# Second half of an output projection, begun beside the last attention head and in the scores' PSUM banks

## The chip, the core and the metric

One core of a Trainium2 chip runs the whole step as one program. The metric is the time of one execution on the device in microseconds (us), the median over runs. The engines of the core are PE (matrix products), DVE and ACT (elementwise work, both read PSUM), POOL and SP (here mostly starters of transfers). PE writes into PSUM, which has eight banks of 128 x 512 numbers in f32.

## The reference

One layer of a streaming encoder on 1024 new rows, 16 meta rows and a sample stream of 32 rows with 512 cached positions (T = 1072 columns in the kernel, the rows being held transposed). Cut to what matters:

```python
mixed = concat(heads_A, heads_B)          # 8 latent heads (MLA), 8 forgetting heads (FoX), 64 wide
x = x + mixed @ w_out                     # output projection, 1024 x 1024
h = rms_norm(x, norm_ffn)
x = x + (silu(h @ w_gate) * (h @ w_up)) @ w_down      # 1024 -> 2816 -> 1024
y = rms_norm(x, norm_final)
```

All products are in f32 quality: an operand is split into a high and a low part (`hi`, `lo`), and each product is three matmuls, hi*hi, hi*lo and lo*hi.

## The kernel before

The program goes through four stages: input projections; the eight forgetting heads (8 to 15 in the code); the eight latent heads (0 to 7); and the rest of the output projection with the feed-forward part. A scheduler of the framework sets the order of the instructions on each engine from the order of the code, from the dependences and from the buffers; it may move an instruction past others that it does not depend on. Each engine then executes its list strictly in that order, and waits on semaphores stand in the list.

**Heads.** `attention` (L725) runs the heads. For each head `scores` (L560) computes nine tiles of scores, L589, into a tile `psS` of two banks, takes the maximum on DVE (L592) and the exponential on ACT (L597). `values` (L619) transposes the probabilities on PE (L651 and L627, into `psT`), copies them on ACT (L67 in the helper `split`, L655), subtracts on DVE (L68, L656), and multiplies by the head's values (L667, L668, L665, L637) into `po`. ACT and DVE bring the sum to `raw` (L675, L678, L680). After each second head `finish_pair` (L684) multiplies by the reciprocal row sums (transposed by L706, product L712) and splits the result into `A_hi` and `A_lo` (L713, L715). The values of a head run behind its scores as a generator, `state["pend"]`, whose steps alternate with the scores of the next group. The values of the last head's second group have nothing behind them, and run out at the end of the stage.

**Filler.** PE would wait in these chains, so a generator of other work is advanced by `fill` (L728). For the latent heads it is `out_half` (L537): the first half of the output projection, over the four blocks `B` of `mixed`, in 48 steps of six matmuls (L551 to L553), added to the input on DVE (L556) and put to DRAM as `sX2`. The rate is 48 steps over 25 x (8 - 0.7) calls; what is left at the start of the last head is run at once (L742).

**Second half.** After the pools of the heads are closed, 24 units (8 blocks of outputs `m`, times the column chunks `FC` of 408, 408 and 256) multiply the blocks `A` of `mixed`, k = 0 to 3, by `w_out` (L845 to L847). Four units at a time do k = 0 to 2 and then k = 3; `A`'s block k = 3 belongs to the last two heads. Their accumulators come from `psG`, a pool of six single banks. DVE adds each to `x2` (L852), which SP loads from `sX2` (eight loads, L820), ACT squares it for the norm (L826, L829), and DVE and ACT make the feed-forward input in the buffers of `A` and `B` (L858, L859) and the factor `rb` (L110 to L116).

**Feed-forward part.** 22 blocks f of 128 hidden columns. For each of the three chunks `gate_up` (L865) makes the gate product and the up product, 24 matmuls each (L121 to L123 in `mm3`), in a bank each; DVE reads the gate bank (L877, times `rb`), ACT takes silu, DVE reads the up bank (L882), multiplies (L883) and splits (L68) into `ah`, `al`. Then `down` (L893) makes the eight down products of the block before, three matmuls each (L889 to L891), in a bank each, and DVE adds each to `x2` (L898). All draw from the six banks of `psG` in turn. DVE also splits the next block's weights (L68, `gl`, `dl`). The last block (f = 21) is laced with the final norm (`down_final`, L923).

```python
psG = C.enter_context(tc.tile_pool(name="psG", bufs=6, space=PSUM))
ps = psG.tile([128, 512], F32, tag="psG", name="psG")      # product(j) of gate_up, L870
```

Of the kernel before, what the change touches and what calls it, by code (L numbers as in the profile page):

```python
# [9 lines left out]
F32 = mybir.dt.float32  # L10
# [39 lines left out]
def trunk(ctx: ExitStack, tc: tile.TileContext, a):  # L50
# [53 lines left out]
    def rows4(t):  # L104
        return t.rearrange("p (k t) -> p k t", k=4)
# [330 lines left out]
    tp = B.enter_context(tc.tile_pool(name="tp", bufs=LAG + 1))  # L436
    st = B.enter_context(tc.tile_pool(name="st", bufs=2))

    psS = B.enter_context(tc.tile_pool(name="psS", bufs=2, space=PSUM))
    psT = B.enter_context(tc.tile_pool(name="psT", bufs=2, space=PSUM))  # L440
    psO = B.enter_context(tc.tile_pool(name="psO", bufs=1, space=PSUM))
    psF = B.enter_context(tc.tile_pool(name="psF", bufs=1, space=PSUM))
# [280 lines left out]
    state = {"pend": iter(()), "n": 0}  # L723

    def attention(hs, filler, steps, last):  # L725
        rate, owed = steps / (25.0 * (len(hs) - 0.7)), [0.0]

        def fill():  # L728
            if last and h == hs[0] and grps[0][0] == 5:
                return  # L730
            owed[0] += rate
            while owed[0] >= 1:
                next(filler, None)
                owed[0] -= 1

        rs = raw = None
        for h in hs:
            nxt = h + 1 if h + 1 < 16 else 0
            if not (last and h == hs[-1]):
                heads[nxt] = 0  # L740
            ops, v = heads.pop(h)
            if h == hs[-1]:  # L742
                for _ in filler:
                    pass
                if not last:
                    masks()
            nops = fetch(nxt) if nxt in heads else None
            if h % 2 == 0:
                rs = st.tile([128, 2, 9], F32, tag="rs", name="rs")
                pool.memset(rs, 1.0)  # L750
                raw = st.tile([128, T], F32, tag="raw", name="raw", bufs=1)
            for grps in (((5, 6, 7, 8),), ((1, 2, 3, 4), (0,))):
                todo = [i for g in grps for i in g]
                P, done = {}, 0
                for j, i in enumerate(todo):
                    P[i] = scores(h, ops, i, rs)
                    fill()
                    while done < (j + 1) * state["n"] // len(todo):
                        next(state["pend"], None)
                        fill()  # L760
                        done += 1
                for _ in state["pend"]:
                    pass
                if nops is not None and len(grps) == 1:
                    heads[nxt] = (nops, fetch_v(nxt))
                gens = [values(h, v, [(i, P[i]) for i in g], raw) for g in grps]
                state["n"] = sum(len(g) + g[0] if g != (0,) else 1 for g in grps)
                if h % 2 == 1 and len(grps) == 2:
                    gens.append(finish_pair(h // 2, rs, raw))
                    state["n"] += 3  # L770
                state["pend"] = chain(*gens)
        for _ in filler:
            pass
# [6 lines left out]
    def masks():  # L780
        B3 = rooms[-1][:106]
        for j, part in enumerate((0, 0, 1)):
            move(B3[32 * j:32 * j + 32], sKR[:, part])
        move(B3[96:106], sMK[0:10])
        mixed["B3"] = B3
# [2 lines left out]
    mixed["A"] = (slot("A_hi"), slot("A_lo"))  # L788

    attention(range(0, 8), out_half(), 48, True)  # L790
    for _ in state["pend"]:
        pass
    B.close()
    hpx.close()
# [2 lines left out]
    with ExitStack() as C:  # L797
# [1 line left out]
        sqp = C.enter_context(tc.tile_pool(name="sqpC", bufs=1, side="right"))  # L799
        ap_ = C.enter_context(tc.tile_pool(name="ap", bufs=2, side="right"))  # L800
        wf = C.enter_context(tc.tile_pool(name="wpf", bufs=2))
        psG = C.enter_context(tc.tile_pool(name="psG", bufs=6, space=PSUM))
        psN = C.enter_context(tc.tile_pool(name="psNF", bufs=2, space=PSUM))

        def ffn_weights(f):
            gh = wf.tile([128, 2, 8, 128], FR, tag="gh", name="gh")
# [23 lines left out]
                marks[1] = eng.tensor_tensor(out=acc[:, cs], in0=acc[:, cs], in1=sq[:, :n], op=ALU.add).ins  # L830

        big = [tuple(rows4(t) for t in mixed[g]) for g in ("A", "B")]
        m_hi, m_lo = big[0]
        W = None
        units = [(m, c) for m in range(8) for c in FC]
        for u0 in range(0, len(units), 4):
            part = []
            for m, (c0, n) in units[u0:u0 + 4]:
                out_weights(8 + m + 2)
                part.append((m, c0, n, psG.tile([128, 512], F32, tag="psG", name="psG"), w_ring[8 + m]))  # L840

            for ks in ((0, 1, 2), (3,)):
                for m, c0, n, ps, w in part:
                    for k in ks:
                        pe.matmul(ps[:, :n], w[0][:, k], m_hi[:, k, c0:c0 + n], start=(k == 0), stop=False)  # L845
                        pe.matmul(ps[:, :n], w[0][:, k], m_lo[:, k, c0:c0 + n], start=False, stop=False)
                        pe.matmul(ps[:, :n], w[1][:, k], m_hi[:, k, c0:c0 + n], start=False, stop=(k == 3))  # L847
            if u0 == 12:
                W = ffn_weights(0)
            for m, c0, n, ps, w in part:  # L850
                cs = slice(c0, c0 + n)
                dve.tensor_tensor(out=x2[:, m, cs], in0=ps[:, :n], in1=x2[:, m, cs], op=ALU.add)  # L852
                square(m, cs, n, dve)
                if m == 7:

                    for k in range(8):
                        hi, lo = (t[:, k % 4, cs] for t in big[k // 4])
                        act.activation(hi, x2[:, k, cs], AF.Copy, scale=g_ffn[:, k:k + 1])  # L858
                        dve.scalar_tensor_tensor(lo, x2[:, k, cs], g_ffn[:, k:k + 1], f32(hi), ALU.mult, ALU.subtract)  # L859
                    ps = psN.tile([128, 512], F32, tag="psn", name="psn")  # L860
                    pe.matmul(ps[:, :n], ones, acc[:, cs], start=True, stop=True)
                    rsqrt(rb[:, cs], ps, n, D, sqp)


        def gate_up(W, c0, n, ah, al, between=None):  # L865
# [1 line left out]
            cs = slice(c0, c0 + n)  # L867

            def product(j):
                ps = psG.tile([128, 512], F32, tag="psG", name="psG")  # L870
                marks[2] = mm3(ps[:, :n], lambda k: gh[:, j, k], lambda k: gl[:, j, k], lambda k: big[k // 4][0][:, k % 4, cs], lambda k: big[k // 4][1][:, k % 4, cs], 8)
                return ps

# [19 lines left out]
        def down(parts, c0, n, norm=False, then=None):  # L893
            cs = slice(c0, c0 + n)
            for m in range(8):
                ps = psG.tile([128, 512], F32, tag="psG", name="psD")
                down_mm(ps[:, :n], m, cs, parts, True, True)
                dve.tensor_tensor(out=x2[:, m, cs], in0=ps[:, :n], in1=x2[:, m, cs], op=ALU.add)  # L898
                if norm:
                    square(m, cs, n, pool if m < 6 else dve)  # L900
                if m == 3 and then is not None:
                    norm_table()
                    final(*then)
# [19 lines left out]
        def down_final(prev, cur, c0, n):  # L923

            cs = slice(c0, c0 + n)
            pairs = [psG.tile([128, 512], F32, tag="psG", name="psD").rearrange("p (a b) -> p a b", a=2) for _ in range(4)]
            for part in (prev, cur):

                with tc.issue_after(marks[2]):
# [159 lines left out]
```

## Time and profile before

| | |
|---|---|
| median of 3 runs | 1538.38 us (1536.78 to 1539.22) |
| the profiled execution | 1537.25 us, span of the trace 1535.5 us |
| PE busy | 1493.0 us (97%), 9317 matmuls |
| DVE busy | 971.5 us (63%) |
| ACT busy | 591.4 us (39%) |
| mean granted clock of PE | 0.993 |
| heads 0 to 7 | about 453 to 689 us |
| rest of the projection | 688.81 to 738.20 us |
| feed-forward part | from 738.20 us |

Times in the trace count from the start of the span. A row of the timeline has the start, the duration, the engine, the line, the operation with output and inputs, and in brackets the engine's idle time before it with what ended it. A matmul's row is longer than the distance to the next, since matmuls are pipelined. PEld is the load of a matmul's weights, which overlaps the matmul before it. The clock is the share of full speed that PE was granted.

### The profile page before, as it was taken

What the parts mean: (1) busy time and instruction counts of PE and PEld (TensorE: products, weight loads), DVE (VectorE), ACT (ScalarE), POOL (GpSimd) and SP (SyncE); (2) the same over time, 40 slices, a digit from 0 to 9 for tenths busy, and PEclk for the clock granted to TensorE, in tenths of its full rate; (3) what the DMA queues carried; (4) which work ended last, traced back from release to release, by engine and by line L of the source; (5) the groups of instructions that cost most, each with busy time, mean ns of one, the idle gap of its engine ahead of it and who ended that gap; (6) DMA issues with size and microseconds to landing.
All of it is one profiled execution on the core that took longest, in us unless ns stands there. A gap on an engine that the chain in (4) does not pass through costs nothing.

```text
span 1535.5 us, 24295 instructions
## 1 busy us (share of the span) xinstructions
PE 1493.0 (97%) x9317; PEld 1433.5 (93%) x9317; DVE 971.5 (63%) x1861; ACT 591.4 (39%) x1198; POOL 198.5 (13%) x331
## 2 busy tenths in 40 slices
PE   9999998999898999989999999999999999999996
PEld 8999997888787898979999999999999999999996
DVE  8874626787966776766855655555555555655547
ACT  7443436777655666654511111111111121111124
POOL 0343242422131211200000000000000000000001
PEclk9999999999999999999999999999999999999999
DMA  6689567778587686515111111111111111111003
GB/s 196 233 258 299 172 210 249 238 218 262 147 238 185 174 212 161 148 41 206 34 50 44 54 42 42 42 42 42 42 42 42 53 58 53 44 42 42 28 1 115
DMA packets 87636, 184.19 MB, mean 120 GB/s; under 512 B 9754, under 2 KB 52954, under 8 KB 87428
## 3 DMA queue, kind: packets, MB, share of 16 engines
q1 hardware_dynamic: 70592, 128.34, 28.8%
q0 software_dynamic: 16928, 54.29, 10.1%
q8 instruction: 74, 1.21, 0.3%
q14 instruction: 42, 0.34, 0.1%
HBM read 123.93 MB, written 58.67 MB: 119 GB/s over the span
## 4 chain that ended last, share of the span: by engine, by line
PE 88%; DVE 4%; ACT 3%; issue 2%; DMA 1%; POOL 1%; DVEq 0%; SPq 0%; POOLq 0%; ACTq 0%
PE psG L122 11%; PE psG L121 11%; PE psG L123 11%; PE psD L890 5%; PE psD L891 5%; PE psD L889 5%; PE psS L589 5%; PE psT L651 4%; PE psA L123 3%; PE psA L121 3%; PE psA L122 3%; PE po L667 2%; PE po L668 2%; PE psA L386 1%; PE psA L387 1%
## 5 line engine op out<-in xcount | busy, mean ns | idle before, releaser
L898 DVE TENSOR_TENSOR x<-psD,x 128x408 f32<-128x408 f32 (+1 forms) x496 | 236.2, 522 | 4.3 <-PE psD L891 4.3
L122 PE MATMUL psG<-B_lo,gh 128*128 128x408 f32 (+1 forms) x528 | 172.8, 327 | 0.0
L121 PE MATMUL psG<-B_hi,gh 128*128 128x408 f32 (+1 forms) x528 | 172.8, 327 | 0.0
L122 PE MATMUL psG<-A_lo,gh 128*128 128x408 f32 (+1 forms) x528 | 172.6, 327 | 0.0
L121 PE MATMUL psG<-A_hi,gh 128*128 128x408 f32 (+1 forms) x528 | 172.3, 326 | 0.0
L891 PE MATMUL psD<-ah,dl 128*128 128x408 f32 (+1 forms) x528 | 172.1, 326 | 0.0
L123 PE MATMUL psG<-B_hi,gl 128*128 128x408 f32 (+1 forms) x528 | 171.8, 325 | 0.0
L123 PE MATMUL psG<-A_hi,gl 128*128 128x408 f32 (+1 forms) x528 | 171.8, 325 | 0.0
L890 PE MATMUL psD<-al,dh 128*128 128x408 f32 (+1 forms) x528 | 171.7, 325 | 0.0
L889 PE MATMUL psD<-ah,dh 128*128 128x408 f32 (+1 forms) x528 | 170.9, 325 | 0.5 <-ACT ah L67 0.5
L878 ACT ACTIVATE sl<-sl 128x408 f32<-128x408 f32 (+1 forms) x66 | 33.1, 503 | 351.3 <-DVE sl L877 351.2
L882 DVE TENSOR_TENSOR sq<-psG,rb 128x408 f32<-128x408 f32 (+1 forms) x66 | 35.0, 530 | 156.5 <-PE psG L123 156.5
L68 DVE TENSOR_TENSOR ptl<-psT,pth 128x512 fp32r<-128x512 f32 x192 | 104.6, 552 | 28.7 <-ACT pth L67 26.6
L592 DVE TENSOR_REDUCE nm<-psS 128x1 f32<-128x656 f32 (+2 forms) x144 | 104.0, 724 | 27.2 <-PE psS L589 25.6
L67 ACT ACTIVATE pth<-psT 128x512 fp32r<-128x512 f32 (+4 forms) x208 | 99.2, 480 | 55.7 <-PE psT L651 46.5
L830 POOL TENSOR_TENSOR acc<-acc,sq 128x408 f32<-128x408 f32 x10 | 10.8, 1076 | 812.4 <-ACT sq L829 811.9
L877 DVE TENSOR_TENSOR sl<-psG,rb 128x408 f32<-128x408 f32 (+1 forms) x66 | 34.9, 530 | 123.0 <-PE psG L123 123.0
L67 ACT ACTIVATE ah<-sl 128x408 fp32r<-128x408 f32 (+1 forms) x66 | 33.2, 503 | 197.2 <-DVE sl L883 125.8
L589 PE MATMUL psS<-b,a 128*128 128x328 f32 (+4 forms) x360 | 99.9, 331 | 7.4 <-ACT pb L597 6.1
L889 PEld LDWEIGHTS psD<-ah,dh 128*128 128x128 f32 x528 | 99.2, 188 | 0.9 <-ACT ah L67 0.7
L122 PEld LDWEIGHTS psG<-B_lo,gh 128*128 128x128 f32 x528 | 99.2, 188 | 0.5 <-issue 0.3
L121 PEld LDWEIGHTS psG<-B_hi,gh 128*128 128x128 f32 x528 | 99.2, 188 | 0.5 <-issue 0.2
(274 smaller groups left out, 3803.5 us busy)
## 6 DMA issues: line engine op xcount, KB each, us to landing
sg<-w_gu SPq DMA_DIRECT2D x44, 512.0 KB
a<-sQ SPq DMA_DIRECT2D x56, 268.0 KB
b<-sK SPq DMA_DIRECT2D x32, 396.0 KB
sg<-w_down SPq DMA_DIRECT2D x22, 512.0 KB
v<-sV SPq DMA_DIRECT2D x16, 512.0 KB
wst<-w_in SPq DMA_DIRECT2D x13, 512.0 KB
sV<-vt POOLq DMA_DIRECT2D x24, 256.0 KB, 4.5
sK<-room POOLq DMA_DIRECT2D x14, 396.0 KB, 4.9
```

The source lines that it names most:

```text
L67: first = act.activation(hi, src, AF.Copy)
L68: return first.ins, eng.tensor_tensor(out=lo, in0=src, in1=f32(hi), op=ALU.subtract).ins
L121: pe.matmul(ps, whi(k), rhi(k), start=(k == 0), stop=False)
L122: pe.matmul(ps, whi(k), rlo(k), start=False, stop=False)
L123: last = pe.matmul(ps, wlo(k), rhi(k), start=False, stop=(k == K - 1))
L589: pe.matmul(out, qa[:K, t0:t0 + nq], kb[:K, k0 + c:k0 + c + w], start=(j == 0), stop=last)
L592: dve.tensor_reduce(out=nm[:nq, j:j + 1], in_=src, axis=AX.XY if len(src.shape) == 3 else AX.X, op=ALU.max, negate=True)
L651: pe.transpose(out=pt[:, 128 * g:128 * g + 128], in_=tiles[g][1][:, c:c + 128], identity=ident)
L889: pe.matmul(ps, dh[:, m], ah[:, cs], start=first and j == 0, stop=False)
L890: pe.matmul(ps, dh[:, m], al[:, cs], start=False, stop=False)
L891: pe.matmul(ps, dl[:, m], ah[:, cs], start=False, stop=last and j == len(parts) - 1)
L898: dve.tensor_tensor(out=x2[:, m, cs], in0=ps[:, :n], in1=x2[:, m, cs], op=ALU.add)
```

## The change

The pool `psS` of the scores, two tiles of two banks, now lives to the end of the program. A generator `begin` draws two of these tiles after the last head and runs k = 0 to 2 of the first four units into their four halves, one step after each step of the last head's values; the later loop does only k = 3 for them. For this the weight slices 8 and 9 of `w_out` are fetched there. `psG` shrinks to two banks, and a function `bank` deals out six banks in turn for everything that drew from `psG`: two halves of a `psS` tile, two halves of the other, two single banks. In `attention` the last range of heads no longer flushes the filler at its last head; its rate is 48 steps over 25 x (8 - 0.25) calls, and the rest runs after the loop.

```diff
-    psS = B.enter_context(tc.tile_pool(name="psS", bufs=2, space=PSUM))
+    psS = ctx.enter_context(tc.tile_pool(name="psS", bufs=2, space=PSUM))
...
-        rate, owed = steps / (25.0 * (len(hs) - 0.7)), [0.0]
+        rate, owed = steps / (25.0 * (len(hs) - (0.25 if last else 0.7))), [0.0]
...
-            if h == hs[-1]:
+            if h == hs[-1] and not last:
                 for _ in filler:
                     pass
-                if not last:
-                    masks()
+                masks()
...
+    def out_products(unit, ps, ks):
+        (m, (c0, n)), w = unit, w_ring[8 + unit[0]]
+        for k in ks:
+            for j, (wj, t) in enumerate(((0, 0), (0, 1), (1, 0))):
+                pe.matmul(ps[:, :n], w[wj][:, k], rows4(mixed["A"][t])[:, k, c0:c0 + n], start=(k == 0 and j == 0), stop=(k == 3 and j == 2))
+
+    early = []
+
+    def begin():
+        for u in (0, 2):
+            out_weights(10)
+            pair = psS.tile([128, 2, 512], F32, tag="psS", name="psS")
+            for j in range(2):
+                early.append(pair[:, j])
+                for k in range(3):
+                    out_products(units[u + j], pair[:, j], (k,))
+                    yield
+
+    begun = begin()
     for _ in state["pend"]:
+        next(begun, None)
+    for _ in begun:
         pass
...
-        psG = C.enter_context(tc.tile_pool(name="psG", bufs=6, space=PSUM))
+        psG = C.enter_context(tc.tile_pool(name="psG", bufs=2, space=PSUM))
...
+        drawn, pair = [4], [None]
+
+        def bank():
+
+            t = drawn[0] % 6
+            drawn[0] += 1
+            if t > 3:
+                return psG.tile([128, 512], F32, tag="psG", name="psG")
+            if t % 2 == 0:
+                pair[0] = psS.tile([128, 2, 512], F32, tag="psS", name="psS")
+            return pair[0][:, t % 2]
...
-                part.append((m, c0, n, psG.tile([128, 512], F32, tag="psG", name="psG"), w_ring[8 + m]))
+                part.append((m, c0, n, early[len(part)] if u0 == 0 else bank(), w_ring[8 + m]))
...
-            for ks in ((0, 1, 2), (3,)):
+            for ks in ((3,),) if u0 == 0 else ((0, 1, 2), (3,)):
...
-                ps = psG.tile([128, 512], F32, tag="psG", name="psG")
+                ps = bank()
```

The last replacement stands in `gate_up`, `down` and `down_final` alike. In the changed program the lines are others: the projection's matmuls are L797, DVE's reads of the gate and the up product L907 and L912, the down products L919 to L921, and DVE's addition to `x2` L928.

The order of the instructions shows at three places what the change moves. In its rows a number behind a name tells one buffer from the next, and the brackets name the semaphores that an instruction waits for (DVE_49 is DVE's count).

PE, end of the last head, before (`po` and `psT` belong to the last head's values, `psG` to the projection):

```order
L665 MATMUL po_8438<-ptm_2591,v_7937 128x512
L706 MATMUL psT_8500<-ident_62,bc_8482 128x128 [waits DVE_49,Pool_49]
L637 MATMUL po_8502<-pth_8464,v_7937 128x96 [waits DMAHW0_49,DVE_49]
L637 MATMUL po_8502<-pth_8464,v_7937 128x96 x4
L845 MATMUL psG_8558<-A_hi_5600,woh_8066 128x408 [waits DVE_49,PE_49]
L846 MATMUL psG_8558<-A_lo_5601,woh_8066 128x408
L847 MATMUL psG_8558<-A_hi_5600,wol_8067 128x408
```

The same stretch with the change, where the first of the 36 products stand:

```order
L667 MATMUL po_8285<-pth_8377,v_7913 128x128 [waits Activation_49]
L668 MATMUL po_8285<-ptl_8378,v_7913 128x128
L797 MATMUL psS_8425<-A_hi_5600,woh_8168 128x408
L797 MATMUL psS_8425<-A_lo_5601,woh_8168 128x408
L797 MATMUL psS_8425<-A_hi_5600,wol_8169 128x408
L651 MATMUL psT_8429<-ident_62,pa_8249 128x128 [waits DVE_49]
L651 MATMUL psT_8429<-ident_62,pa_8296 128x128
L651 MATMUL psT_8429<-ident_62,pa_8326 128x128
L665 MATMUL po_8285<-ptm_2591,v_7913 128x512 [waits DMAHW4_49,DMAHW3_49,Pool_49]
L797 MATMUL psS_8425<-A_hi_5600,woh_8168 128x408
L797 MATMUL psS_8425<-A_lo_5601,woh_8168 128x408
L797 MATMUL psS_8425<-A_hi_5600,wol_8169 128x408
```

The projection's products now stand between the transposes and value products of the last head, and those of its first two units are in one tile, psS_8425.

PE in the third chunk of a feed-forward block, from the gate product's end to the up product, before:

```order
L122 MATMUL psG_10434<-B_lo_2594,gh_9906 128x256
L123 MATMUL psG_10434<-B_hi_2593,gl_9907 128x256
L121 MATMUL psG_10461<-A_hi_5600,gh_9906 128x256 [waits DVE_49]
L122 MATMUL psG_10461<-A_lo_5601,gh_9906 128x256
L123 MATMUL psG_10461<-A_hi_5600,gl_9907 128x256
```

With the change (psS_10386 holds the gate product in its first half and the up product in its second; `ah` and `dh` are those of the down products):

```order
L123 MATMUL psS_10386<-B_hi_2593,gl_9876 128x256
L919 MATMUL psG_10441<-ah_9891,dh_9575 128x256 [waits Activation_49]
L920 MATMUL psG_10441<-al_9892,dh_9575 128x256
L921 MATMUL psG_10441<-ah_9891,dl_9576 128x256
L919 MATMUL psG_10446<-ah_9891,dh_9575 128x256
L920 MATMUL psG_10446<-al_9892,dh_9575 128x256
L121 MATMUL psS_10386<-A_hi_5600,gh_9875 128x256 [waits DVE_49]
L122 MATMUL psS_10386<-A_lo_5601,gh_9875 128x256
```

Five matmuls of down products now stand between gate and up, and the up product's first matmul waits for DVE. The count that it waits for is that of L907, which reads the gate half of the same tile.

PE at the end of a block, the last down products and the next block's gate product, before:

```order
L889 MATMUL psD_10520<-ah_9922,dh_9596 128x256 [waits DVE_49]
L890 MATMUL psD_10520<-al_9923,dh_9596 128x256
L891 MATMUL psD_10520<-ah_9922,dl_9597 128x256
L889 MATMUL psD_10525<-ah_9922,dh_9596 128x256 [waits DVE_49]
L890 MATMUL psD_10525<-al_9923,dh_9596 128x256
L891 MATMUL psD_10525<-ah_9922,dl_9597 128x256
L121 MATMUL psG_10550<-A_hi_5600,gh_10218 128x408 [waits DVE_49]
```

With the change (psS_10451 and psS_10460 are the two tiles of two banks; each appears here for its second half, psS_10499 is the tile of the next block's gate):

```order
L920 MATMUL psG_10469<-al_9892,dh_9575 128x256
L921 MATMUL psG_10469<-ah_9891,dl_9576 128x256
L919 MATMUL psG_10474<-ah_9891,dh_9575 128x256 [waits DVE_49]
L920 MATMUL psG_10474<-al_9892,dh_9575 128x256
L921 MATMUL psG_10474<-ah_9891,dl_9576 128x256
L919 MATMUL psS_10451<-ah_9891,dh_9575 128x256 [waits DVE_49]
L920 MATMUL psS_10451<-al_9892,dh_9575 128x256
L921 MATMUL psS_10451<-ah_9891,dl_9576 128x256
L919 MATMUL psS_10460<-ah_9891,dh_9575 128x256 [waits DVE_49]
L920 MATMUL psS_10460<-al_9892,dh_9575 128x256
L921 MATMUL psS_10460<-ah_9891,dl_9576 128x256
L121 MATMUL psS_10499<-A_hi_5600,gh_10177 128x408 [waits DVE_49]
```

The second halves of two tiles stand last. Each waits for the reader of its tile's first half, and the gate product behind them waits for the readers of psS_10451, whose banks it takes over.

## Rows read from the trace of the kernel before

**Rows 1.** Busy us (count) of PE, PEld, DVE, ACT, POOL; granted clock, DMA share, GB/s
```profile
487.40:651.40 164.00, 160.73 (x1054) 147.46 (x1053) 116.38 (x223) 104.64 (x249) 35.97 (x63) 1.00 0.69 179
651.40:676.00 24.60, 23.06 (x148) 20.35 (x147) 17.49 (x33) 15.09 (x37) 1.62 (x3) 1.00 0.10 34
676.00:689.00 13.00, 8.80 (x54) 6.74 (x53) 9.33 (x20) 6.73 (x16) 1.84 (x6) 0.91 0.03 8
689.00:700.00 11.00, 11.00 (x53) 10.87 (x54) 2.51 (x7) 1.47 (x4) 0.00 (x0) 0.79 0.99 392
738.20:1450.00 711.80, 711.80 (x4333) 709.73 (x4332) 410.45 (x801) 133.36 (x202) 0.00 (x0) 1.00 0.13 44
```

**Rows 2.** Table of waits, PE, 676 to 689.3: total us, times, longest
```profile
PE psG L845 <- DVE raw L712: 1.1, 1, 1.1
PE po L637 <- DVE raw L678: 0.9, 1, 0.9
PE psT L651 <- DVE ptl L68: 0.6, 2, 0.4
PE psT L706 <- DVE ptm L656: 0.5, 1, 0.5
PE psT L651 <- DVE ptm L656: 0.5, 1, 0.5
PE po L667 <- DVE raw L678: 0.4, 1, 0.4
```

**Rows 3.** Timeline of PE: first and last of 13 matmuls, start and us
```profile
688.81 0.68 PE L845 MATMUL psG<-A_hi,woh 128*128 128x408 f32 x1 [1.10 <-DVE raw L712]
...
693.37 0.43 PE L846 MATMUL psG<-A_lo,woh 128*128 128x408 f32 x1
```

**Rows 4.** Timeline of DVE and PE, a PE restart after a wait
```profile
680.09 0.69 DVE L678 TENSOR_TENSOR raw<-po,half 64x512 f32<-64x512 f32 x1
...
680.83 0.50 PE L667 MATMUL po<-pth,v 128*128 128x512 f32 x1 [0.42 <-DVE raw L678]
...
681.16 0.39 PE L668 MATMUL po<-ptl,v 128*128 128x512 f32 x1
```

**Rows 5.** Timeline, a 408-column down product and its reader
```profile
772.78 0.35 PE L890 MATMUL psD<-al,dh 128*128 128x408 f32 x1
...
772.97 0.35 PE L891 MATMUL psD<-ah,dl 128*128 128x408 f32 x1
...
773.35 0.58 DVE L898 TENSOR_TENSOR x<-psD,x 128x408 f32<-128x408 f32 x1
```

**Rows 6.** Timeline, third chunk (256 columns): up's end, DVE's steps behind it
```profile
796.05 0.28 PE L123 MATMUL psG<-B_hi,gl 128*128 128x256 f32 x1
...
796.17 0.28 PE L889 MATMUL psD<-ah,dh 128*128 128x256 f32 x1
...
796.37 0.42 DVE L882 TENSOR_TENSOR sq<-psG,rb 128x256 f32<-128x256 f32 x1 [2.43 <-PE psG L123]
...
796.73 0.42 DVE L898 TENSOR_TENSOR x<-psD,x 128x256 f32<-128x256 f32 x1
...
797.07 0.42 DVE L883 TENSOR_TENSOR sl<-sl,sq 128x256 f32<-128x256 f32 x1
```

**Rows 7.** Timeline of SP's queue: the loads of x2
```profile
687.74 3.92 SPq L58 DMA_DIRECT2D x<-sX  x8
```

**Rows 8.** Timeline of DVE: first read of a gate product; a weight split
```profile
752.55 0.57 DVE L877 TENSOR_TENSOR sl<-psG,rb 128x408 f32<-128x408 f32 x1
...
800.17 1.22 DVE L68 TENSOR_TENSOR dl<-sg,dh 128x1024 fp32r<-128x1024 f32 x1 [0.37 <-ACT dh L67]
```

**Rows 9.** Timeline, last chunk: gate's end, its reader, PE's wait for ah
```profile
1512.04 0.28 PE L123 MATMUL psG<-B_hi,gl 128*128 128x256 f32 x1
...
1514.06 0.42 DVE L877 TENSOR_TENSOR sl<-psG,rb 128x256 f32<-128x256 f32 x1
...
1518.49 0.39 PE L889 MATMUL psD<-ah,dh 128*128 128x256 f32 x1 [0.49 <-ACT ah L67]
```

More of the change, by code (lines that the diff above doesn't have):

```diff
@@ L790, in trunk @@
     attention(range(0, 8), out_half(), 48, True)
+    units = [(m, c) for m in range(8) for c in FC]
+    def out_products(unit, ps, ks):
[14 more added lines that the diff above has]
+    begun = begin()
     for _ in state["pend"]:
+        next(begun, None)
+    for _ in begun:
         pass
@@ L832, in trunk @@
         big = [tuple(rows4(t) for t in mixed[g]) for g in ("A", "B")]
-        m_hi, m_lo = big[0]
         W = None
-        units = [(m, c) for m in range(8) for c in FC]
         for u0 in range(0, len(units), 4):
@@ L839, in trunk @@
                 out_weights(8 + m + 2)
-                part.append((m, c0, n, psG.tile([128, 512], F32, tag="psG", name="psG"), w_ring[8 + m]))
-            for ks in ((0, 1, 2), (3,)):
[L843 to L847, printed above, removed]
+                part.append((m, c0, n, early[len(part)] if u0 == 0 else bank(), w_ring[8 + m]))
+            for ks in ((3,),) if u0 == 0 else ((0, 1, 2), (3,)):
+                for j, (m, c0, n, ps, w) in enumerate(part):
+                    out_products(units[u0 + j], ps, ks)
             if u0 == 12:
@@ L895, in down @@
             for m in range(8):
-                ps = psG.tile([128, 512], F32, tag="psG", name="psD")
+                ps = bank()
                 down_mm(ps[:, :n], m, cs, parts, True, True)
@@ L925, in down_final @@
             cs = slice(c0, c0 + n)
-            pairs = [psG.tile([128, 512], F32, tag="psG", name="psD").rearrange("p (a b) -> p a b", a=2) for _ in range(4)]
+            pairs = [bank().rearrange("p (a b) -> p a b", a=2) for _ in range(4)]
             for part in (prev, cur):
```

## The prediction

> **What bounds the kernel now.** I read the busy time by stretch first. From 738.20 to 1450 us, nearly all of the feed-forward part, PE is busy in the whole stretch at full clock, DVE in 410 of 712 us [rows 1]: nothing is to be gained there, and every wait that PE gets there lengthens the kernel. The heads before it are nearly as full (160.73 of 164.00). The hole is where the attention ends: 8.80 busy of 13.00 us, then eleven at a mean granted clock of 0.79 [rows 1]. The table of waits says what PE lacks there: steps of the last head's values that go PE to ACT to DVE and back, six kinds of wait of 4.0 us together [rows 2]. When the projection can start, its matmuls begin 0.35 us apart, 13 from 688.81 to 693.37 [rows 3], where later ones of that size are 0.185 apart [rows 5]: the clock had fallen to its lower level, 1.2 GHz, while PE was short of work.
>
> **The change, part by part.** The sums are made against the profiled execution, 1537.25 us (span 1535.5), which lies 1.1 under the median of the three runs, 1538.38.
>
> *Products in the tail.* Thirty-six matmuls of the projection (27 of 408 columns, 9 of 256) are issued between the last head's steps; at 0.185 [rows 5] and 0.12 us [rows 6] they are 6.1 us, and the order shows that nearly all stand ahead of the last L637. The 4.0 us of idle are really some 5.1, because a matmul's row runs 0.16 past the point where the next could begin (0.35 long, 0.185 apart) [rows 5], seven times. What stays is the end of the chain, 1.1 us of waiting for the last L712 [rows 2], which the k = 3 products need as well. I take 4.0 gained. With PE busy the clock should hold: 13 matmuls in 4.56 us [rows 3] would take 2.4, so 2.1 more. Bounds: 2 (the products delay the chain, the clock still falls) and 8.
>
> *The filler of the first half.* The lower rate takes about 3 steps of 6 matmuls, 2.9 us, from seven heads with 3.3 us of idle, and spreads them and the four that were flushed at the start of the last head over that head, which has 1.5 [rows 1]. If those seven are held up by other engines when PE has less, they stay as long as they were; PE's total is the same. From +1 lost to 1.5 gained; I take 0.3 lost. Stage in all: 6 gained.
>
> *Weights and loads.* The two slices of weights that come earlier are one ACT and one DVE step each, where both have idle. The eight loads of x2 stay behind L637 in SP's queue [rows 7] and, of 549 KB each at 392 GB/s [rows 1], land one per 1.4 us. After L637 PE has 33 matmuls, some 5.3 us, before it asks for a bank whose reader needs the first load; that lands about 3 us after L637. Nothing.
>
> *Banks of the feed-forward part.* Here is the cost. Before, six single banks go round. Now four of the six are halves of two-bank tiles, and the order shows what this adds: the first matmul into a second half waits for DVE, and its count is that of the step that reads the *first* half. The tile is guarded as a whole, so PE may not write bank 1 while DVE still has to read bank 0; and a pair can be drawn again only when both halves were read. DVE reads a bank a few steps late, which six banks hid.
>
> The round trip, from the start of a half's last matmul to the first into the other half: DVE begins 0.38 us later and takes 0.58 [rows 5], PE restarts 0.05 after DVE's end (680.78 to 680.83), and that first matmul takes 0.11 longer than its like, 0.50 for 0.39 [rows 4], its weights not being loaded ahead. Sum 1.1 us. With 256 columns: 0.32 and 0.42 [rows 6], so 0.9. The cover is what stands between, at 0.185 or 0.12 a matmul: five of 408 just do, seven of 256.
>
> The order gives 408-column pairs five between, or more. They lose only where DVE has queued reads: about 0.15 us in the first two chunks. The third chunk, zero at the gate's or the up product's last matmul:
> - up half: five between, due at 0.71, free at 0.89: 0.18.
> - the first half of the pair that the gate and up held (psS_10460 in the order): five between, 0.18.
> - second half of psS_10451: DVE has four steps 0.34 apart [rows 6], so its first half is read from 1.35 to 1.77 and PE may go at 1.92; due at 1.83: 0.09.
> - next block's gate, into that same pair: the second half ends at 2.16, is read from 2.48 to 2.90, free at 3.05; due at 2.63: 0.42.
>
> That is 0.87, with the 0.15 some 1.0 us a block, and the 20 blocks f = 1 to 20 repeat it: 20 us. Below, all covered, 0. Above: if each of the ten pair waits of a block lost the 0.1 us by which the cover is uncertain, 1.0 more, 40 us in all.
>
> At the start, no gate product can be read before the norm's factor rb; the first is read 14.35 us after the first gate matmul (752.55 in rows 8, 738.20). Nobody waited for that. Now the first chunk's up half does. PE has the other gate products and the third chunk to do first, 48 + 48 matmuls and the norm sums, about 16 us; DVE's order now puts two weight splits of 1.2 us [rows 8] ahead of that read, which ends at 14.35 + 2.4 + 0.58, so PE may go at some 17.5. DVE's own chain moves up by less than PE's, too: I take 2 lost, between 0 and 3.5. At the end the last chunk's gate is read 2.0 us after its last matmul [rows 9], behind the final norm's steps (row 1514.06 after 1512.04), and the up half now waits for it: 2.0 + 0.42 + 0.16, some 2.5, of which the 0.49 that PE later waits for ah [rows 9] comes back; two more pair waits with longer chains before it, 1.0. I take 3, between 1 and 5.
>
> Feed-forward in all +25, stage before it -6: +19, 1556 us.
>
> The Trainium skill's page "PSUM — Partial Sum Buffer" (PSUM bank collisions raise a hardware error) has the guard per bank and quadrant, and says that two engines on different banks run clean; by that the waits of second halves need not be, and the sum would be 1537.25 - 6 = 1531. The order shows them in the program all the same, and PE serves what the program waits for.
>
> **Rivals.**
> - *All waits covered* (the other side). One mechanism: DVE's reads are back before PE gets there. It decides at a round trip of 0.7 us with 256 columns, against 0.9 summed above, and with DVE's queue no longer than one read. Then only start and end are left, at the low bounds: 1537.25 - 6 + 1 = 1532. For it: DVE is 58% busy here. Against: its work stands in bunches, four steps without a gap after each up product [rows 6].
> - *More waits than counted.* If the cover of the 408 pairs falls 0.1 short everywhere, a block loses 1.6 to 2: 1568 to 1576.
> - *The tail gains nothing*: products sit ahead of chain steps and the clock falls anyway, 2 gained for 6: 1560.
> - *The clock falls in the feed-forward part*, as before 688.81, once in each block: 20 times the 2.1 us of the tail, 42 more, 1598. Against it: from 651.40 to 676.00 PE was idle 1.5 of 24.6 us at a granted clock of 1.00 [rows 1], more than 1.0 in 36. The Trainium skill's page "TensorE: Matmul & The Clock Gate" (A second HAM failure mode: psum-queue depth-cycling) says that a PE which pauses again and again for its banks can swing between the two levels. By that rule this is the outcome; the trace of the heads speaks against it.
> - *The change does not do what it says*: the order shows that it does.
>
> **How the numbers follow.** Forecast 0.78, covered 0.07, more waits 0.08, no gain in the tail 0.04, clock 0.03. The forecast's own range is 1548 to 1564: 0.6 to 1.3 us a block, with the stage's bounds. It holds the weak tail; down to 1546 and up to 1568 takes in the edge of the covered case and of more waits, and leaves out under 2 in 10. A measurement here tells about 0.2%, 3 us, from nothing. Faster 0.05 and same 0.02 are the covered case, slower 0.93 the rest.
>
> **What would show it.** Right: between the last scores and the projection's k = 3 products one wait of about 1 us and the granted clock at 1.00; the feed-forward block 36.3 us long instead of the 35.3 that its 144 matmuls of 408 and 72 of 256 columns take; a table of PE's waits for that part, empty of entries before, with DVE's L907, L912 and L928 as releasers, some 20 us, most at the next block's first gate matmul; one wait of about 2 us near 750 and one of 2 to 3 in the last chunk. Wrong: a block that keeps its length, or a half-clock stretch there. If the block is longer and the total is not, the tail was worth more than 6.

## The result, and the profile after

| | before | with the change |
|---|---|---|
| median | 1538.8 us (4 runs) | 1559.5 us (4 runs, 1557.64 to 1562.26) |
| ratio | | 1.0138, 95% interval 1.0126 to 1.0150 |
| profiled execution | 1537.25 us, span 1535.5 | 1557.64 us, span 1555.6 |
| mean granted clock of PE | 0.993 | 0.992 |

The change makes the kernel 19 to 23 us slower; forecast were 1556, 19 us slower, with a range of 1546 to 1568. Both sides of the sum, the gain and the price, can be seen in the trace; two of its terms were off, in opposite directions.

The end of the heads first. Busy time by stretch with the change, columns as in [rows 1]:

```profile
651.40:676.00 24.60, 23.96 (x156) 21.69 (x155) 17.97 (x35) 15.82 (x38) 2.46 (x6) 1.00 0.10 34
676.00:689.00 13.00, 12.64 (x86) 11.44 (x83) 8.44 (x15) 5.88 (x12) 1.54 (x5) 1.00 0.17 41
689.00:700.00 11.00, 10.07 (x59) 10.08 (x60) 5.43 (x14) 4.00 (x9) 0.00 (x0) 1.00 0.97 390
738.20:1450.00 711.80, 707.00 (x4227) 686.81 (x4226) 405.36 (x775) 123.94 (x185) 0.00 (x0) 1.00 0.14 44
```

The hole is filled: 12.64 of 13.00 us busy where it was 8.80, with 86 matmuls for 54, and in the eleven microseconds after it a granted clock of 1.00 for 0.79 [rows 1]. What is left is the end of the chain: one wait of 1.2 us for the last L712, as there was before [rows 2]. It lies from 688.7 to 689.9, mostly in the third row. The table of waits, PE, 676 to 700 us, with the change:

```profile
PE psG L797 <- DVE raw L712: 1.2, 1, 1.2
```

The last row of the stretches is the price: in the feed-forward part PE does 4227 matmuls in the time in which it did 4333.

The table of waits shows only a part of that loss. PE from 738 to 1560 us, with the change (columns: us in total, times, longest):

```profile
PE psS L121 <- DVE sl L907: 4.9, 2, 3.2
PE psS L121 <- DVE x L928: 3.2, 20, 0.2
PE psS L919 <- DVE x L928: 1.7, 2, 0.8
PE psn L950 <- DVE acc L865: 0.3, 1, 0.3
```

This is 10 us, and 28 are lost (2.2, 19.3 and 6.3 us, the terms of the feed-forward part that are measured further below). The row of a matmul runs on beyond the point where the next could begin, so a short wait hides in the row of the matmul before it, and one of under 0.16 us doesn't appear at all. The view of line L928 shows more of it, under those who waited for it:

```profile
  PEld psS L121: 7.3, 20
```

The weight load of each block's first gate matmul stood 0.37 us, twenty times; PE's own row shows 0.17 of it. The safe measure is the distance between the same two instructions in both traces. These are the first gate matmul of block f = 2 and that of f = 21, before:

```profile
799.00 0.35 PE L121 MATMUL psG<-A_hi,gh 128*128 128x408 f32 x1
...
1471.11 0.35 PE L121 MATMUL psG<-A_hi,gh 128*128 128x408 f32 x1
```

and with the change:

```profile
794.50 0.46 PE L121 MATMUL psS<-A_hi,gh 128*128 128x408 f32 x1 [0.17 <-DVE x L928]
...
1484.92 0.45 PE L121 MATMUL psS<-A_hi,gh 128*128 128x408 f32 x1 [0.17 <-DVE x L928]
```

Nineteen blocks took 672.11 us and take 690.42: 35.37 and 36.34 each, so 0.96 more. Behind 1471.11 the span went on for 64.4 us, behind 1484.92 for 70.7: 6.3 more.

One such wait, at the end of a block with the change (PE's and DVE's rows):

```profile
866.67 0.78 DVE L928 TENSOR_TENSOR x<-psS,x 128x256 f32<-128x256 f32 x2
866.70 0.28 PE L921 MATMUL psS<-ah,dl 128*128 128x256 f32 x1
...
867.14 0.45 PE L121 MATMUL psS<-A_hi,gh 128*128 128x408 f32 x1 [0.16 <-DVE x L928]
...
867.44 0.34 PE L122 MATMUL psS<-A_lo,gh 128*128 128x408 f32 x1
```

DVE reads two second halves in a row (one row, x2). The gate product takes over the tile of the first, and starts 0.44 us after the last down matmul where 0.12 is the rule [rows 6], the matmul behind it 0.30 later where 0.19 is [rows 5]: 0.43 lost.

### The profile page after: what moved, and what is told of

Read it like the earlier page. It is cut to its first block, busy times and chain, and to the rows that moved or that the text cites. A ratio compares the mean times of both kernels' runs of the same rounds, so it can differ in the third digit from the quotient of the medians.

```text
span 1555.6 us, 24245 instructions
## 1 busy us (share of the span) xinstructions
PE 1509.2 (97%) x9317; PEld 1429.3 (92%) x9317; DVE 981.4 (63%) x1861; ACT 591.1 (38%) x1198; POOL 198.6 (13%) x331
## 4 chain that ended last, share of the span: by engine, by line
PE 87%; DVE 7%; ACT 3%; issue 2%; DMA 1%; POOL 1%; SPq 0%; DVEq 0%; ACTq 0%; POOLq 0%
PE psS L121 8%; PE psS L122 7%; PE psS L123 7%; PE psS L589 5%; PE psT L651 4%; PE psG L121 4%; PE psS L919 4%; PE psG L123 4%; PE psG L122 4%; PE psS L921 3%; PE psS L920 3%; PE psA L121 3%; PE psA L122 3%; PE psA L123 3%; PE po L667 2%; PE po L668 2%
## 5 line engine op out<-in xcount | busy, mean ns | idle before, releaser
L928 DVE TENSOR_TENSOR x<-psS,x 128x408 f32<-128x408 f32 (+1 forms) x330 | 172.1, 541 | 39.2 <-PE psS L921 38.2
L121 PE MATMUL psS<-A_hi,gh 128*128 128x408 f32 (+1 forms) x360 | 119.5, 332 | 8.1 <-DVE sl L907 4.9
L592 DVE TENSOR_REDUCE nm<-psS 128x1 f32<-128x656 f32 (+2 forms) x144 | 104.1, 725 | 28.3 <-PE psS L589 26.7
L919 PE MATMUL psS<-ah,dh 128*128 128x408 f32 (+1 forms) x348 | 119.9, 344 | 1.7 <-DVE x L928 1.7
L920 PE MATMUL psS<-al,dh 128*128 128x408 f32 (+1 forms) x348 | 115.2, 331 | 0.0
L921 PE MATMUL psS<-ah,dl 128*128 128x408 f32 (+1 forms) x348 | 115.0, 331 | 0.0
L122 PE MATMUL psS<-B_lo,gh 128*128 128x408 f32 (+1 forms) x360 | 114.7, 319 | 0.0
L122 PE MATMUL psS<-A_lo,gh 128*128 128x408 f32 (+1 forms) x360 | 114.5, 318 | 0.0
L121 PE MATMUL psS<-B_hi,gh 128*128 128x408 f32 (+1 forms) x360 | 114.4, 318 | 0.0
L123 PE MATMUL psS<-A_hi,gl 128*128 128x408 f32 (+1 forms) x360 | 114.3, 318 | 0.0
L123 PE MATMUL psS<-B_hi,gl 128*128 128x408 f32 (+1 forms) x360 | 113.8, 316 | 0.0
L912 DVE TENSOR_TENSOR sq<-psS,rb 128x408 f32<-128x408 f32 (+1 forms) x45 | 22.9, 509 | 113.0 <-PE psS L123 113.0
L928 DVE TENSOR_TENSOR x<-psG,x 128x408 f32<-128x408 f32 (+1 forms) x166 | 79.6, 499 | 1.0 <-PE psG L921 1.0
```

Source lines behind the costliest of these rows:

```text
L121: pe.matmul(ps, whi(k), rhi(k), start=(k == 0), stop=False)
L122: pe.matmul(ps, whi(k), rlo(k), start=False, stop=False)
L123: last = pe.matmul(ps, wlo(k), rhi(k), start=False, stop=(k == K - 1))
L919: pe.matmul(ps, dh[:, m], ah[:, cs], start=first and j == 0, stop=False)
L920: pe.matmul(ps, dh[:, m], al[:, cs], start=False, stop=False)
L921: pe.matmul(ps, dl[:, m], ah[:, cs], start=False, stop=last and j == len(parts) - 1)
```

## The experiments

Three marks cut each trace into the parts of the sum: the first matmul of the filler `out_half` (463.05 us before, 462.55 with the change), the first gate matmul of f = 2, and that of f = 21. The table is worked out from these three rows and the span of each profiled execution.

| kernel | filler's start to f = 2 | one block | f = 21 to the end | median us | ratio to before, 95% |
|---|---|---|---|---|---|
| before | 335.95 | 35.37 | 64.4 | 1538.08, 1537.54 | |
| the change | 331.95 | 36.34 | 70.7 | 1559.5 | 1.0138 (1.0126 to 1.0150) |
| change, six single banks | 328.76 | 35.37 | 64.4 | 1532.19 | 0.9966 (0.9954 to 0.9978) |
| before, pairs | 332.44 | 36.33 | 70.5 | 1559.63 | 1.0139 (1.0125 to 1.0152) |
| before, pool split 4 + 2 | 328.41 | 35.37 | 64.4 | 1532.35 | 0.9964 (0.9951 to 0.9976) |
| before, new filler | 333.25 | 35.37 | 64.4 | 1537.07 | 0.9989 (0.9981 to 0.9998) |
| change, halves apart | 329.31 | 35.73 | 64.7 | 1540.67 | 1.0021 (1.0013 to 1.0030) |
| change, ends in single banks | 332.63 | 36.34 | 69.1 | 1557.85 | 1.0128 (1.0109 to 1.0148) |
| before, split and filler | 328.49 | 35.37 | 64.4 | 1533.64 | 0.9973 (0.9961 to 0.9984) |

The kernel before ran again beside each group: its first median belongs to the four rows from single banks to new filler, its second to the last three. What lies ahead of the first mark differs by up to 4 us between the nine traces (462.55 to 466.76), so parts are compared from mark to mark. Each trace is one execution; the medians and their intervals say how far a difference between traces can be trusted.

**The change with six single banks.** The early products stay in the scores' tiles; behind the first four units the pool is closed and its four banks are taken singly.

```diff
-    psS = ctx.enter_context(tc.tile_pool(name="psS", bufs=2, space=PSUM))
+    S4 = ctx.enter_context(ExitStack())
+    psS = S4.enter_context(tc.tile_pool(name="psS", bufs=2, space=PSUM))
...
-            if t % 2 == 0:
-                pair[0] = psS.tile([128, 2, 512], F32, tag="psS", name="psS")
-            return pair[0][:, t % 2]
+            return psH[0].tile([128, 512], F32, tag="psH", name="psG")
...
         for u0 in range(0, len(units), 4):
+            if u0 == 4:
+                S4.close()
+                psH[0] = C.enter_context(tc.tile_pool(name="psH", bufs=4, space=PSUM))
```

(`psG` and `psN` are put at the other end of PSUM, with `side="right"`, so that the pool can be closed before them.)

> The change, but from the fifth unit of the projection on the four banks of the scores are handed to a pool of four single banks, so that six single banks go round again; the 36 early products stay. Theory A (the loss is the guard of a two-bank tile as a whole): the 27.5 us that PE loses after 700 us against the kernel before go away and the 7.5 us won at the end of the heads stay, 1538.8 - 7.5 = 1531, a feed-forward block of 35.36 us. Theory B (the loss comes from moving products forward: the order of DVE's and ACT's work behind them shifts, the banks are only the place where it shows): 1555 to 1560, blocks of 36.3 us.

Measured: 1532.19 us, blocks of 35.37. Theory A holds, theory B falls. Its stretches:

```profile
676.00:689.00 13.00, 12.88 (x88) 11.88 (x87) 8.28 (x15) 5.99 (x13) 2.07 (x7) 1.00 0.12 37
...
738.20:1450.00 711.80, 711.80 (x4336) 710.43 (x4334) 405.95 (x790) 128.12 (x189) 0.00 (x0) 1.00 0.14 45
```

The tail is as full as with the change, and the feed-forward part does 4336 matmuls for 4227. PE writes one bank there while DVE reads the next, without a lost microsecond, so it was not the banks' being neighbours that cost time. The Trainium skill's page "PSUM — Partial Sum Buffer" (PSUM bank collisions raise a hardware error), by which engines on different banks run clean, agrees with this trace, which adds that it cost no time: 35.37 us a block here and before.

**The kernel before with pairs.** Nothing of the change but the way of drawing banks, in a pool of its own.

```diff
-        psG = C.enter_context(tc.tile_pool(name="psG", bufs=6, space=PSUM))
+        psH = C.enter_context(tc.tile_pool(name="psH", bufs=2, space=PSUM))
+        psG = C.enter_context(tc.tile_pool(name="psG", bufs=2, space=PSUM))
...
+            if t > 3:
+                return psG.tile([128, 512], F32, tag="psG", name="psG")
+            if t % 2 == 0:
+                pair[0] = psH.tile([128, 2, 512], F32, tag="psH", name="psH")
+            return pair[0][:, t % 2]
```

> The kernel before with one thing of the change: behind the heads, four of the six banks are drawn as two tiles of two banks (a pool of its own, where the scores were), dealt out in the change's order. No generator, no new rate of the filler. Its order of PE shows that first products of the projection go up between the last head's steps here too, since the banks of the new pool are those of the scores alone. Theory A: as slow as the change, 1556 to 1562, blocks of 36.3 us, first products before 688 us. Theory B (moving products by the generator, with the slices of weights, costs the time): no more than the kernel before, 1531 to 1539.

Measured: 1559.63 us, the change's own time, and the same table of waits to a tenth (PE, 700 to 1560 us):

```profile
PE psH L121 <- DVE sl L890: 4.9, 2, 3.2
PE psH L121 <- DVE x L911: 3.3, 20, 0.2
PE psH L902 <- DVE x L911: 1.7, 2, 0.8
PE psn L933 <- DVE acc L843: 0.3, 1, 0.3
```

Pairs alone make the loss. This kernel has no generator, and its part up to f = 2 is nevertheless as short as the change's.

**The kernel before with its pool split.** Only this, four single banks where the scores were, and two:

```diff
-        psG = C.enter_context(tc.tile_pool(name="psG", bufs=6, space=PSUM))
+        psH = C.enter_context(tc.tile_pool(name="psH", bufs=4, space=PSUM))
+        psG = C.enter_context(tc.tile_pool(name="psG", bufs=2, space=PSUM))
...
+            t = drawn[0] % 6
+            drawn[0] += 1
+            if t > 3:
+                return psG.tile([128, 512], F32, tag="psG", name="psG")
+            return psH.tile([128, 512], F32, tag="psH", name="psH")
```

> The kernel before with psG split into a pool of four single banks (in the place of the scores) and one of two. Nothing else. In PE's order the first products go up between the last head's steps, as in the pair version, with single banks. Theory A: the gain of the stage without the loss, 1538.8 - 6 to 8 = 1531 to 1533. Rival C (the gain of the stage needs the generator that laces products by hand and the later flush of the filler): 1535 to 1539. Against the pair version the difference is the price of the guard: A expects 25 to 29 us.

Measured: 1532.35 us. The stretch of the tail, the first of the projection's products, the last value products, and PE's waits from 676 to 700 us:

```profile
676.00:689.00 13.00, 12.21 (x81) 10.48 (x81) 8.76 (x17) 6.50 (x16) 1.83 (x6) 1.00 0.01 3
...
679.41 0.45 PE L856 MATMUL psH<-A_hi,woh 128*128 128x408 f32 x1 [0.47 <-ACT pa L597]
...
688.12 0.66 PE L637 MATMUL po<-pth,v 112*128 112x96 f32 x5
...
PE psH L856 <- ACT pa L597: 0.5, 1, 0.5
PE psT L706 <- DVE ptm L656: 0.3, 1, 0.3
```

The scheduler puts the first products between the last head's steps by itself: 12.21 us busy for 8.80, clock 1.00. Eighteen of the projection's matmuls, all of 408 columns, stand ahead of the last L637, where the generator puts 33. The products that are left run on behind it, and the wait for the last L712, which the change keeps, is gone. Against the pairs it is 27.3 us faster (1559.63 - 1532.35); the two traces are 28.3 us apart, of which 4.0 lie up to f = 2, 18.2 in the nineteen blocks and 6.1 behind them. Rival C falls: the gain needs neither the generator nor the later flush. Why the old pool of six kept the products back is argued, not shown: it covered banks of the scores and of `psT`, `po` or `psF`, which are free only after the last value step; that a split alone lets them go up is shown.

**The kernel before with the new filler.** Rate and flush as in the change, nothing else.

```diff
-        rate, owed = steps / (25.0 * (len(hs) - 0.7)), [0.0]
+        rate, owed = steps / (25.0 * (len(hs) - (0.25 if last else 0.7))), [0.0]
...
-            if h == hs[-1]:
+            if h == hs[-1] and not last:
```

> The kernel before with the change's filler alone: the lower rate in the latent heads, no flush at the start of the last head. My prediction's term: between 1 lost and 1.5 gained, 1537.5 to 1540. Rival C (most of the 7.5 us of the stage come from the filler that runs on into the last head): 1532 to 1535.

Measured: 1537.07 us, 0.9989 (0.9981 to 0.9998), so 0.3 to 2.9 us gained. In this trace the projection starts at 692.02, 3.2 us later than before [rows 3], so the stretches of its tail are taken 3.2 us later too:

```profile
679.20:692.20 13.00, 8.88 (x60) 7.26 (x59) 9.22 (x19) 7.06 (x16) 2.38 (x7) 1.00 0.17 44
692.20:703.20 11.00, 11.00 (x68) 10.97 (x68) 3.71 (x8) 2.24 (x5) 0.00 (x0) 1.00 1.00 397
```

The hole is as large as before (8.88 us busy, for 8.80), though the filler now runs into its start: the last of its matmuls begins at 680.76, before at 657.67. Yet the granted clock is 1.00 in both stretches, where it was 0.91 and 0.79 [rows 1]. In this trace the clock's 2 us are thus had with the filler alone, without the hole being filled; why the clock holds here is not shown.

**Split and filler together.** The two edits above in one kernel.

```diff
-        rate, owed = steps / (25.0 * (len(hs) - 0.7)), [0.0]
+        rate, owed = steps / (25.0 * (len(hs) - (0.25 if last else 0.7))), [0.0]
...
+            return psH.tile([128, 512], F32, tag="psH", name="psH")
```

> The kernel before with psG split into four and two single banks, as in the run before, and the change's filler; no generator. If the filler's gain (0.1%) and that of the split add up: 1530 to 1531. If both fill the same hole at the end of the heads, which then holds nothing more: 1532, as the split alone and as the change with single banks.

Measured: 1533.64 us, 0.9973 (0.9961 to 0.9984), as the split alone; up to f = 2 it takes 328.49 us for 328.41. They don't add up: with either alone the granted clock behind the hole is already 1.00, and that can be won only once.

**The change with the halves further apart.** The same tiles and the same guard, drawn in another turn.

```diff
-            if t > 3:
+            if t % 3 == 2:
                 return psG.tile([128, 512], F32, tag="psG", name="psG")
-            if t % 2 == 0:
-                pair[0] = psS.tile([128, 2, 512], F32, tag="psS", name="psS")
-            return pair[0][:, t % 2]
+            if t < 2:
+                pair[t] = psS.tile([128, 2, 512], F32, tag="psS", name="psS")
+            return pair[t % 3][:, t // 3]
```

> The change with another turn of the same six banks: first half of the one tile, first half of the other, a single bank, then the second halves and the other single bank, so that two whole banks, six matmuls or more, lie between a tile's halves. The tiles, their guard and all products are the same. If the price is the round trip to DVE's reader less what stands between the halves (1.1 us less five matmuls of 0.12 in the third chunk, 0.9 to 1.1 for six to eight), two thirds of it or more go: blocks of 35.5 to 35.8 us for 36.3, and the first and the last chunk's waits of 1.9 and 3.5 us go too, since the reader's own product is then further back: 1536 to 1543 in all. If it is the pair as such that costs (each second half waits a fixed time, wherever it stands): as the change, 1556 to 1562.

Measured: 1540.67 us, blocks of 35.73, the last part 64.7 us. Of 0.96 us a block 0.36 are left (a little under two thirds are gone), of 6.3 at the end 0.3, and the wait at the start is gone (329.31). The price is the round trip less its cover, then, and not the pair as such. About half of what is left in a block is shown by these rows, the rest is three waits of under 0.1 us:

```profile
863.59 0.42 DVE L912 TENSOR_TENSOR sq<-psS,rb 128x256 f32<-128x256 f32 x1 [2.42 <-PE psS L123]
...
863.86 0.28 PE L920 MATMUL psG<-al,dh 128*128 128x256 f32 x1
...
864.07 0.38 PE L919 MATMUL psS<-ah,dh 128*128 128x256 f32 x1
...
864.29 0.28 PE L920 MATMUL psS<-al,dh 128*128 128x256 f32 x1
```

The up product's reader ends at 864.01, PE restarts 0.06 later, 0.21 after the matmul before instead of 0.12, and the next follows 0.22 later: 0.19 lost, the same size as one of the waits that I had summed for pairs.

**The change with the ends in single banks.** The turn is moved on for the first chunk of the first block and the last chunk of the last.

```diff
         for f in range(NFF):
             Wn = ffn_weights(f + 1) if f + 1 < NFF else None
+            if f < 2:
+                drawn[0] += (4, 2)[f]
...
+                drawn[0] += 2
                 with tc.issue_after(exp):
                     gate_up(W, *FC[2], *cur[1:], rest)
```

> The change, but the turn of the banks is moved on so that the gate and the up product of the first chunk of the first block, and of the last chunk of the last block, lie in the two single banks. The blocks 1 to 20 stay as they are. My terms for start and end: the wait of 1.9 us at 749 us and the wait of 3.5 us at 1528 us go, and with the latter the stretch behind it in which matmuls of 256 columns begin 0.21 us apart instead of 0.12 (16 of them, 1.5 us): 6.5 less, 1553. Rival (what PE does not wait there it waits a little later, for ah or for the norm): start gains 0 to 1, end 1 to 3, 1556 to 1558.

Measured: 1557.85 us, where the rival had put it (1556 to 1558). The times of its four runs overlap those of the change, so it is the parts of the trace that decide: up to f = 2 nothing is gained (332.63 for 331.95), at the end 1.6. PE's waits, 700 to 1560 us:

```profile
PE psS L121 <- DVE x L928: 3.3, 20, 0.2
PE psS L919 <- ACT ah L67: 1.7, 1, 1.7
PE psS L919 <- DVE x L928: 1.7, 2, 0.9
PE psG L121 <- DVE x L882: 1.4, 1, 1.4
```

The wait of 1.7 us at the start has become one of 1.4 for a single bank, whose reader is still adding the projection to `x2` (L882); the wait of 3.2 us at the end has become one of 1.7 for `ah`. So at the start PE now waits for another reader than before, and at the end for the next link of the same chain. Taking the pair away at these two places moved the waits and made them somewhat shorter; it did not remove them.

## Why the prediction was right, and where not

The forecast came out (1559.5 for 1556), and its step that carries most holds: the guard of a two-bank tile, 0.96 us a block. That the total is only 1.6 off is in part luck: the last block cost 3.3 more than was taken, and the end of the heads gave 1.2 more. The terms by the marks:

| term | forecast | measured | from |
|---|---|---|---|
| end of the heads | -6 | -7.2 | 335.95 to 328.76, the change with single banks |
| start of the feed-forward part | +2 | +2.2 | 331.95 - 328.76, less one block's 0.96 |
| 20 blocks | +20 | +19.3 | 36.34 - 35.37 |
| last block | +3 | +6.3 | 70.7 - 64.4 |
| sum | +19 | +20.6 | the spans differ by 20.1, the start of the filler by -0.5 |

The marks are those of one execution each. By the medians the change with single banks is 5.9 us faster than before (3.4 to 7.1), so the gain at the end of the heads is known no better than that.

- *The blocks.* The four waits of the third chunk were put at 0.18, 0.18, 0.09 and 0.42. The trace (the block that ends with the rows at 866.67 above) has 0.19 at the up half, 0.19 at the first half of the pair that the gate and the up product held, 0.05 at the second half of the other pair, 0.43 at the next gate, and some 0.13 at the larger chunks for the 0.15 that I took. The sign that I had named for it did not show: not some 20 us in the table of waits, most at the next gate, but 10, with 3.2 there. A sum of such small terms holds because each is a duration of a row less a count of matmuls from the order.
- *The tail.* The holes were worth about what was said: less the clock's 2.1, the split alone gained 5.4 (7.5 from 335.95 to 328.41), for the 4.0 that were taken and the 1.1 of the last wait, which it fills as well. The filler was worth more: "I take 0.3 lost", bounds 1 lost and 1.5 gained, and alone it shortens the part by 2.7 (335.95 to 333.25). Two of these are the clock's, which I had put wholly to the products. By the medians the filler gained 1.0 (0.3 to 2.9), so how much of the 2.7 it gains in most executions is not shown. Since products and filler win the same 2 us, the total of the stage is only 1.2 off.
- *The start.* The wait is there, 1.72 us at 749.26, with the two weight splits ahead of the reader as the order had shown: the second of them begins at 747.16 (1.22 us), and the read at 748.63:

```profile
748.63 0.57 DVE L907 TENSOR_TENSOR sl<-psS,rb 128x408 f32<-128x408 f32 x1
...
749.26 0.46 PE L121 MATMUL psS<-A_hi,gh 128*128 128x408 f32 x1 [1.72 <-DVE sl L907]
```

  In the run with the ends in single banks a wait of 1.4 us on another bank took its place, and with the halves apart there was none (329.31): it hangs on the turn in which the banks are dealt.
- *The last block* is the step that failed: 3, with bounds of 1 and 5, for 6.3. The mechanism stood in the text, the sizes did not. "Two more pair waits ... 1.0" are 1.0 each, at 1515.06 and 1523.81. The wait of the up half is 3.5 for 2.5, because the gate's reader on DVE stands behind four more steps of the norm (seven for three) and begins 4.2 us after the gate's last matmul, where 2.0 was taken from [rows 9]:

```profile
1526.57 0.28 PE L123 MATMUL psS<-B_hi,gl 128*128 128x256 f32 x1
...
1530.78 0.42 DVE L907 TENSOR_TENSOR sl<-psS,rb 128x256 f32<-128x256 f32 x1
...
1531.25 0.58 PE L121 MATMUL psS<-A_hi,gh 128*128 128x256 f32 x1 [3.16 <-DVE sl L907]
```

  And behind this wait came something that the forecast left out, a lower clock:

```profile
1527.50:1531.20 3.70, 0.58 (x2) 0.00 (x0) 3.70 (x9) 2.37 (x3) 0.00 (x0) 1.00 0.11 43
1531.20:1534.70 3.50, 3.45 (x16) 3.45 (x17) 2.64 (x5) 0.42 (x1) 0.00 (x0) 0.51 0.53 193
1534.70:1541.00 6.30, 6.30 (x55) 6.30 (x55) 3.77 (x7) 2.44 (x4) 0.00 (x0) 1.00 0.36 133
```

  After 3.7 us with two matmuls the granted clock is 0.51, the level of 1.2 GHz, for 3.5 us, in which 16 matmuls begin some 0.21 us apart; at 1.00 they would have taken 16 x 0.12 = 1.9. So 1.5 of the 6.3 are the clock's. I priced the clock where the change removed a wait, and not where it added one.
- *The rivals.* That all waits are covered falls with 36.34 us a block, and so does that far more of them are open (a loss of 1.6 to 2 a block). That the tail gains nothing falls with 7.2 us and a granted clock of 1.00. That the clock swings in the feed-forward part falls too: twenty waits, and a granted clock of 1.00 from 738.20 to 1450. The Trainium skill's page "TensorE: Matmul & The Clock Gate" (A second HAM failure mode: psum-queue depth-cycling) says that it can swing where PE pauses again and again for its banks; with some 1.0 us of pauses in each block of 36, this trace does not show it.

## What to carry to other kernels

A tile is the unit of waiting: in this framework a two-bank tile whose halves are filled by different products makes the second wait for the reader of the first, though with single banks in the same place no such wait was needed (35.37 us a block). What that costs is the round trip to the reader less the work that stands between the halves; take single banks, or draw the halves far apart (0.96 us a block became 0.36). And before work is laced into a hole by hand, see whether a pool that spans too much keeps it out: two smaller pools in place of one gave the whole gain here, 1532.35 us for 1538.1, with none of the loss.

## What the runs showed of the hardware that I had not expected

- With the filler alone PE was busy 8.88 of the 13.00 us up to the projection, with waits of up to 1.4 us, and the granted clock stayed at 1.00; before, with 8.80 of 13.00 and waits of up to 1.1 us, it had fallen when the projection began [rows 1 to 3].
- After single waits it did not fall every time: at 749.26, behind 1.72 us of waiting, the next 4 us were granted 1.00, and the last block's row above had 0.51 behind 3.16; with the ends in single banks a wait of 1.7 us for `ah` was followed by 0.57:

```profile
1538.70:1542.70 4.00, 3.96 (x18) 3.80 (x19) 2.32 (x5) 1.35 (x2) 0.00 (x0) 0.57 0.48 175
```

Neither the length of one wait nor the busy time of the stretch parts these cases; what does stays open.
